# An encoder's first stage: small inputs as rows, a sine in another place, and a loop whose order is written out by hand

## The chip, the cores and the metric

The kernel runs on one core of a Trainium2 chip. The core has five engines with queues of their own, here under the names that the profile gives them: TensorE (PE, matmuls; PEld is its loading of weights), VectorE (DVE), ScalarE (ACT), GpSimd (POOL) and SyncE (SP), whose queue issues the loads and stores. The metric is the device time of one execution in microseconds, the median of several runs. A profiled execution is one more run, whose trace gives each instruction's start and duration from the start of the span.

## The reference

Two layers of an encoder on a sequence of 512 positions with a width of 1024, in f32. Each layer gets six modulation vectors from a conditioning vector `c`: shift, scale and gate for the attention half and for the MLP half. `rope` turns parts of queries and keys by angles that come from the positions.

```
c_act = silu(c)
for l in range(2):
    mod = c_act @ w_mod[l] + b_mod[l]              # 6 x 1024
    sh1, sc1, gt1, sh2, sc2, gt2 = split(mod, 6)
    h = rms_norm(x, g_norm_mix[l]) * (1 + sc1) + sh1
    q_d, k_d, v_d, cq, ckv, k_rope = split(h @ w_in[l])      # 1952 columns
    o_dil = dilated_attention(rms_norm(q_d), rms_norm(k_d), v_d, positions)   # 8 heads, bias by distance
    o_mla = latent_attention(cq, ckv, k_rope, positions, ...)                 # 8 heads, rope on 32 dims
    x = x + gt1 * (concat[o_dil, o_mla] @ w_out[l])
    h = rms_norm(x, g_norm_mlp[l]) * (1 + sc2) + sh2
    x = x + gt2 * (relu(h @ w_mlp_in[l]) ** 2 @ w_mlp_out[l])
```

## The kernel before

x lies transposed: eight tiles `xT[j]` of 128 features by 512 positions. To keep f32's precision, each operand of a large product is split in a rounded high part and a low part that is the rest, and three matmuls add up to one product (`mm3`, L240). `load_split` (L229) does this for weights: a load into a buffer `raw` or `zz`, a copy on ScalarE (`wh`, L233) and a subtraction on GpSimd (`wl`, L234). `raw` has three buffers, `zz` two, `wh` and `wl` four each.

The kernel is written as a program in one order. A planner places each engine's instructions by a model of their times, and may move them past each other where the data allow it; the buffers of a tag are handed on as they come free. Three things limit the planner: `keep_in_program_order` holds one instruction behind what stands before it on its engine, `issue_after` puts all that follows on an engine behind an instruction, and inside a `manual_schedule` block the named engines keep the written order. Before, that block names VectorE alone.

The first stage, which the change touches, goes so:

1. Small loads: `c` as a tile `cs` of 128 x 8, an identity matrix, `cols` (biases and gains), the positions `posc` as 128 x 4, the rotary frequencies `inv`, then the eight tiles of x (L86 to L99).
2. silu of c, with an exponential on ScalarE (L107), spread to all 128 partitions as `cb` by two matmuls and two copies (L111 to L118).
3. The sum of squares of x: ScalarE squares (L124, L127), VectorE adds (L128).
4. Sine and cosine of the rotary angles: thirteen operations on GpSimd reduce the angles (L135 to L145), ScalarE takes an absolute value, GpSimd turns it into the cosine's argument, and ScalarE takes two sines (L150, L151). Then ScalarE's tables for logarithm and exponential are loaded again (L152), and every later instruction of ScalarE stands behind that.
5. The chunk loop (L750 to L780) over the eight chunks k of 128 features. For each chunk two modulation blocks, k (shift) and 8 + k (scale), of 128 x 1024 are multiplied by `cb` and summed on VectorE (`mod_block`, L170), ScalarE adds the biases (`first_norm`, L194 and L195), VectorE multiplies x by the norm's factor `y` (`u_of`, L768 and L759), ScalarE makes the high part of h (L772) and, in a second pass, the unrounded h (L773). The low part of h is a subtraction, for even chunks on VectorE (L763), for odd ones on GpSimd (L775). Every second chunk loads weights of two groups, `win` (768 columns) and `winc` (832 columns). TensorE adds each chunk's 24 matmuls to eight accumulators: 128 x 384 of the first pair of heads, 128 x 416 of the latent projections, for four blocks of positions.
6. The norm's factor (`inv_rms`, L249): TensorE sums over partitions into `p` (L753), VectorE makes a scaled copy `v` (L251), ScalarE takes logarithm (L252) and exponential (L253, over `p`), and three operations of VectorE refine it (L254 to L256).
7. Behind the loop: the norms of q and k (`do_chain`), the turning by TensorE (`tail`), the same for the latent part with the tables of the rotary part (`rope_tables`, L504, and L554 to L562, ten plus four operations on GpSimd and two loads), and the tables of position differences (`distances`, L309). Then eight stages of heads follow (`heads`), where the matmuls of the next stage are woven in by numbers in `TUNE`.

Of the kernel before, what the change touches and what calls it, by code (L numbers as in the profile page):

```python
# [16 lines left out]
L = 2  # L17
D = 1024
# [24 lines left out]
def trunk(ctx: ExitStack, tc: tile.TileContext, a):  # L43
# [42 lines left out]
    cs = col(8, "cs")  # L86
    SY.dma_start(cs, a["c"].rearrange("(k p) -> p k", p=128))
    ident = const.tile([128, 128], F32, name="ident")
    SY.dma_start(ident, a["ident"])
    cols = [col(N_COL, f"cols{l}") for l in range(L)]  # L90
    SY.dma_start(cols[0], a["cols"][0])
    posc = const.tile([128, 4], I32, name="posc")
    SY.dma_start(posc, a["pos"].rearrange("(t p) -> p t", p=128))
    inv = col(16, "inv")
# [9 lines left out]


    e = small(8)
    A.activation(e, cs, AF.Exp, scale=-1.0)  # L107
    V.tensor_scalar(e, e, 1.0, None, op0=OP.add)
    V.reciprocal(e, e)
    V.tensor_tensor(cs, cs, e, op=OP.mult)  # L110
# [20 lines left out]
    pf = col(4, "pf")  # L131
    V.tensor_copy(pf, posc)
    ang, kf, w_ = s2([128, 4, 16]), s2([128, 4, 16]), s2([128, 4, 16], tag="b")
# [12 lines left out]
    A.activation(kf, ang, AF.Abs)  # L146
    G.tensor_scalar(kf, kf, -1.0, math.pi / 2, op0=OP.mult, op1=OP.add)
    sin = const.tile([128, 4, 16], F32, name="sin")
    cos = const.tile([128, 4, 16], F32, name="cos")
    A.activation(sin, ang, AF.Sin)  # L150
    A.activation(cos, kf, AF.Sin)  # L151
    pre = A.preload_act_table_set("natural_log_exp_and_others")  # L152
    tc.keep_in_program_order(pre)
    ctx.enter_context(tc.issue_after(pre.ins))
# [94 lines left out]
    def inv_rms(p, v, y, t):  # L249

        V.tensor_scalar(v, p, 1.0 / D, EPS, op0=OP.mult, op1=OP.add)  # L251
        A.activation(t, v, AF.Ln)  # L252
        A.activation(p, t, AF.Exp, scale=-0.5)  # L253
        V.tensor_tensor(t, v, p, op=OP.mult)  # L254
        V.scalar_tensor_tensor(t, t, -0.5, p, op0=OP.mult, op1=OP.mult)
        V.scalar_tensor_tensor(y, t, 1.5, p, op0=OP.add, op1=OP.mult)  # L256
# [52 lines left out]
    def distances():  # L309
# [3 lines left out]
        part = []  # L313
        for src, n, tile_ in ((posr, S, lambda dt: t4("pt", [128, 2, S], dt)),
                              (posc, 4, lambda dt: const.tile([128, 2, 4], dt, name=nm("pc")))):
            it, ft = tile_(I32), tile_(F32)
            V.tensor_scalar(it[:, 0], src, 16, None, op0=OP.arith_shift_right)
            V.tensor_scalar(it[:, 1], src, 65535, None, op0=OP.bitwise_and)
            V.tensor_copy(ft, it)
            part.append(ft)  # L320
        row, clm = part
# [66 lines left out]
    for l in range(L):  # L388
# [131 lines left out]
        def latent():  # L520
# [20 lines left out]
            def tail():  # L541
                cn = lat["cn"]
                lat["CT"] = []
                for i in range(3):
# [8 lines left out]
                    lat["CT"].append(ct)  # L553
                lat["Cq"], lat["Sq"] = rope_tables(a["gqr"][l], 0)  # L554
# [9 lines left out]
            w["tail"] = tail  # L564
# [169 lines left out]
        if l == 0:  # L734
# [15 lines left out]
            with tc.manual_schedule(engines={mybir.EngineType.DVE}):  # L750
                for k in range(-1, 8):
                    if k < 0:
                        T.matmul(p, ones, sq0, start=True, stop=True)  # L753
                    elif k % 2 == 0:
                        PR[0]["load"][k // 2](raw=("raw", "zz")[k // 2 % 2])
                        W["load"][k // 2](raw=("raw", "zz")[k // 2 % 2])
# [7 lines left out]
                    if k < 7:  # L764
                        mod_block(0, k + 1, "ot", out=mraw[:, k + 1:k + 2])
                        if k < 0:
                            inv_rms(p, v, y, t)
                            V.tensor_tensor(u_of(0), xT[0], y, op=OP.mult)  # L768
# [5 lines left out]
                        if k % 2 == 0:  # L774
                            G.tensor_tensor(lo, u_of(k + 1), f(hi), op=OP.subtract)  # L775
                    if k >= 0:
                        for tb in range(4):
                            PR[0]["step"](banks[tb][:, :384], k, tb)
                        for tb in range(4):
                            W["step"](lbanks[tb][:, :W_C], k, tb)  # L780
            gains()
# [12 lines left out]
        else:  # L794
# [9 lines left out]
            run(ev + [(tn("W0"), PR[0]["tail"][0]), (tn("W1"), PR[0]["tail"][1]), (tn("W2"), W["tail"])])  # L804

        for st in range(8):
# [19 lines left out]
            if st == 7:  # L826
                ev += spread([lambda jj=jj: out_load(1, jj) for jj in range(4)], tn("OL0"), tn("OL1"))
                ev += [(tn("OE") + j, lambda j=j: early(j)) for j in range(3)]
            if l == 0:
# [159 lines left out]
```

## Time and profile before

| | |
|---|---|
| median of 3 runs | 1345.82 us (1344.32 to 1347.77) |
| the profiled execution | 1343.71 us |
| its span | 1341.6 us |
| TensorE busy in the span | 1263.8 us, 94% |
| VectorE, ScalarE, GpSimd busy | 57%, 51%, 49% |
| moved by the DMA queues | 167.62 MB, mean 125 GB/s |
| mean granted clock of TensorE | 0.984 |

A line of a timeline gives start and duration in us, the engine, the line of the kernel, the operation, what is written and read, shapes, the count of merged instructions, and in brackets the idle time before it with what ended it. A line of a group gives busy us and mean ns of one behind the first bar, and idle us with what ended most of it behind the second. A line by stretch gives the stretch, its length, busy us (count) of PE, PEld, DVE, ACT and POOL, then granted clock, DMA share and GB/s.

### The profile page before, as it was taken

How to read it: one execution, taken by the hardware profiler on the slowest of the kernel's cores; microseconds unless marked ns; L12 is line 12 of the kernel's file. 1: busy time of each engine (PE TensorE's matmuls, PEld its weight loads, DVE VectorE, ACT ScalarE, POOL GpSimd, SP SyncE). 2: the span in 40 equal slices, each digit the busy share in tenths (PEclk: the TensorE clock that was granted, in tenths of full speed). 3: DMA queues.
4: the chain of work that ended last, by engine and by line, in shares of the span. 5: the costliest groups of instructions: out<-in, count | busy, mean ns of one | idle time of the engine just before them, and what ended most of it. 6: DMA issues, size and time to landing. Idle time of an engine off the chain costs nothing.

```text
span 1341.6 us, 19641 instructions
## 1 busy us (share of the span) xinstructions
PE 1263.8 (94%) x7114; PEld 1108.2 (83%) x7114; DVE 762.4 (57%) x1644; ACT 679.8 (51%) x1421; POOL 652.0 (49%) x504
## 2 busy tenths in 40 slices
PE   4879988988999999999999999899899999999998
PEld 2878867877998888888899999798799888888888
DVE  6777797886763661834476678987672121121223
ACT  5567898777632322322237677887663232232321
POOL 5646876674534444444438333545452444444441
PEclk7989999999999999999999999999999999999999
DMA  9335543332254572844434244211121222232221
GB/s 340 113 100 174 184 156 110 105 122 69 79 176 166 192 250 95 278 166 161 166 121 131 77 135 123 86 48 63 40 72 64 95 95 96 96 106 96 94 95 64
DMA packets 57248, 167.62 MB, mean 125 GB/s; under 512 B 8640, under 2 KB 10816, under 8 KB 57152
## 3 DMA queue, kind: packets, MB, share of 16 engines
q1 hardware_dynamic: 57152, 166.38, 37.2%
q8 instruction: 56, 0.92, 0.3%
q14 instruction: 40, 0.33, 0.1%
HBM read 155.87 MB, written 10.49 MB: 124 GB/s over the span
## 4 chain that ended last, share of the span: by engine, by line
PE 75%; DVE 6%; ACT 5%; DMA 3%; POOL 3%; issue 2%; DVEq 0%; ACTq 0%; POOLq 0%
PE mm L241 22%; PE mm L244 22%; PE mm L245 22%; PE tr L377 3%; PE tr L365 2%; DMA raw<-in_wout_dram 1%; DVE pt L371 1%; POOL wl L234 1%; DVE P L350 1%; ACT P L354 1%; PE sc L241 1%; ACT wh L233 1%; POOL raw L167 1%; PE sc L244 1%; PE sc L492 1%
## 5 line engine op out<-in xcount | busy, mean ns | idle before, releaser
L234 POOL TENSOR_TENSOR wl<-raw,wh 128x1024 fp32r<-128x1024 f32 (+3 forms) x174 | 395.2, 2273 | 434.4 <-ACT wh L233 431.1
L233 ACT ACTIVATE wh<-raw 128x1024 fp32r<-128x1024 f32 (+3 forms) x174 | 174.7, 1004 | 264.7 <-PE mm L245 212.0
L670 DVE SCALAR_TENSOR_TENSOR x<-mm,mod,x 128x512 f32<-128x512 f32 (+1 forms) x152 | 92.4, 621 | 255.1 <-PE mm L245 254.5
L241 PE MATMUL mm<-h,wh 128*128 128x512 f32 (+1 forms) x544 | 198.3, 364 | 0.0
L244 PE MATMUL mm<-h,wl 128*128 128x512 f32 (+1 forms) x544 | 198.1, 364 | 0.0
L245 PE MATMUL mm<-h,wh 128*128 128x512 f32 (+1 forms) x544 | 197.9, 364 | 0.0
L241 PE MATMUL mm<-ot,wh 128*128 128x512 f32 (+1 forms) x416 | 147.1, 354 | 0.8 <-DVE x L670 0.4
L865 ACT ACTIVATE P<-mm 128x512 f32<-128x512 f32 (+1 forms) x80 | 41.0, 513 | 210.3 <-PE mm L245 206.8
L245 PE MATMUL mm<-ot,wh 128*128 128x512 f32 (+1 forms) x416 | 143.7, 349 | 1.5 <-POOL ot L663 1.5
L244 PE MATMUL mm<-ot,wl 128*128 128x512 f32 (+1 forms) x416 | 144.9, 349 | 0.0
L866 DVE SCALAR_TENSOR_TENSOR mm<-mm,P 128x512 f32<-128x512 f32 (+1 forms) x80 | 46.9, 589 | 135.7 <-ACT P L865 135.7
L241 PEld LDWEIGHTS mm<-h,wh 128*128 128x128 f32 x544 | 102.7, 189 | 16.3
L244 PEld LDWEIGHTS mm<-h,wl 128*128 128x128 f32 x544 | 102.7, 189 | 16.1
L245 PEld LDWEIGHTS mm<-h,wh 128*128 128x128 f32 x544 | 102.6, 189 | 16.2
L241 PE MATMUL mm<-qk,wh 128*128 128x512 f32 (+1 forms) x288 | 105.3, 366 | 1.0 <-DVE x L670 1.0
L244 PE MATMUL mm<-qk,wl 128*128 128x512 f32 (+1 forms) x288 | 105.3, 365 | 0.0
L245 PE MATMUL mm<-qk,wh 128*128 128x512 f32 (+1 forms) x288 | 105.2, 365 | 0.0
L170 DVE SCALAR_TENSOR_TENSOR pt<-pt,cb 128x1024 f32<-128x1024 f32 x56 | 100.7, 1828 | 0.0
L371 DVE TENSOR_TENSOR pt<-tr,pt 128x512 fp32r<-128x512 f32 x128 | 86.6, 684 | 18.1 <-ACT pt L370 17.5
L362 POOL TENSOR_SCALAR P<-P,hs 128x512 f32<-128x512 f32 x64 | 48.1, 751 | 99.9 <-DVE hs L355 81.0
L241 PE MATMUL mm<-wh,h 128*128 128x384 f32 x240 | 81.3, 353 | 11.7 <-ACT h L772 9.8
L365 PE MATMUL tr<-ident,P 128*128 128x128 f32 x512 | 77.5, 275 | 15.7 <-DVE o L381 6.1
(290 smaller groups left out, 2968.9 us busy)
## 6 DMA issues: line engine op xcount, KB each, us to landing
raw<-in_w_dram SPq DMA_DIRECT2D x64, 512.0 KB, 3.4
pt<-in_wmod_dram SPq DMA_DIRECT2D x56, 512.0 KB, 4.8
raw<-in_w2a_dram SPq DMA_DIRECT2D x48, 512.0 KB, 3.5
raw<-in_wmod_dram SPq DMA_DIRECT2D x24, 512.0 KB, 3.6
raw<-in_win_dram SPq DMA_DIRECT2D x30, 384.0 KB, 3.0
bias<-b SPq DMA_DIRECT2D x32, 256.0 KB, 2.1
raw<-in_wout_dram SPq DMA_DIRECT2D x16, 512.0 KB, 3.7
raw<-in_w2b_dram SPq DMA_DIRECT2D x16, 512.0 KB, 3.4
```

Source lines behind the costliest of these rows:

```text
L170: r = V.scalar_tensor_tensor(w, w, 1.0, cb, op0=OP.mult, op1=OP.mult, accum_out=out)
L233: ra = A.activation(hi, raw, AF.Copy)
L234: rg = G.tensor_tensor(lo, raw, f(hi), op=OP.subtract)
L241: r = T.matmul(out, sh, mh, start=first, stop=False)
L244: T.matmul(out, sl, mh, start=False, stop=False)
L245: T.matmul(out, sh, ml, start=False, stop=last)
L362: G.tensor_scalar(P, P, r_, 0.0, op0=OP.mult, op1=OP.add)
L365: T.transpose(tr[:, kc], P[:, kc * 128:(kc + 1) * 128], ident)
L371: V.tensor_tensor(lo, tr, f(hi), op=OP.subtract)
L670: V.scalar_tensor_tensor(xT[j][:, hf], p, gt[:, j:j + 1], xT[j][:, hf], op0=OP.mult, op1=OP.add)
L865: A.activation(r, p, AF.Relu)
L866: V.scalar_tensor_tensor(p, p, 0.0, r, op0=OP.max, op1=OP.mult)
```

## The change

The small inputs `c` and positions are loaded as rows (8 x 128 and 4 x 128, one partition per row) and turned by TensorE, through a PSUM bank; the split of the positions into two halves is done on the rows and turned with them, and `distances` no longer does it. The tables for logarithm and exponential are loaded at the start and a second time behind the chunk loop, by `exp_tables`. The cosine's argument is made by two operations on VectorE, sine and cosine are one operation on ScalarE, and it stands in the chunk loop at k = 0. The logarithm of `inv_rms` reads the sum `p` itself. `manual_schedule` names VectorE, GpSimd, ScalarE and SyncE. The first pair of weight loads moves behind the norm's factor. The rotary part of the latent tail becomes an event of its own, in the first layer at place 2 of the second stage of heads. In `distances` two pairs of buffers become one, with the conversion in place.

```diff
@@ -83,15 +83,15 @@
         return const.tile([128, n], F32, name=nm(name))
-    cs = col(8, "cs")
-    SY.dma_start(cs, a["c"].rearrange("(k p) -> p k", p=128))
-    ident = const.tile([128, 128], F32, name="ident")
+    rows = s2([8, 4, 128], tag="b")
+    crow, prow, pi = rows[:, 0], rows[:4, 1].bitcast(I32), rows[:4, 2:].bitcast(I32)
+    cs, ident, inv = col(8, "cs"), col(128, "ident"), col(16, "inv")
+    cols = [col(N_COL, f"cols{l}") for l in range(L)]
+    SY.dma_start(crow, a["c"].rearrange("(k p) -> k p", k=8))
     SY.dma_start(ident, a["ident"])
-    cols = [col(N_COL, f"cols{l}") for l in range(L)]
+    SY.dma_start(prow, a["pos"].rearrange("(t p) -> t p", t=4))
     SY.dma_start(cols[0], a["cols"][0])
-    posc = const.tile([128, 4], I32, name="posc")
-    SY.dma_start(posc, a["pos"].rearrange("(t p) -> p t", p=128))
-    inv = col(16, "inv")
     SY.dma_start(inv, bass.AP(tensor=a["inv"].tensor, offset=a["inv"].offset, ap=[[0, 128], [1, 16]]))
     xT = [const.tile([128, S], F32, name=f"x{j}") for j in range(8)]
@@ -102,12 +102,20 @@
     epsc = col(1, "eps")
     V.memset(epsc, EPS)
+    def exp_tables():
+        pre = A.preload_act_table_set("natural_log_exp_and_others")
+        tc.keep_in_program_order(pre)
+        ctx.enter_context(tc.issue_after(pre.ins))
+    exp_tables()
     e = small(8)
-    A.activation(e, cs, AF.Exp, scale=-1.0)
+    turn = ps("mm")
+    T.transpose(turn[:, :8], crow, ident[:8, :8])
+    A.activation(e, turn[:, :8], AF.Exp, scale=-1.0)
     V.tensor_scalar(e, e, 1.0, None, op0=OP.add)
     V.reciprocal(e, e)
-    V.tensor_tensor(cs, cs, e, op=OP.mult)
+    V.tensor_tensor(cs, turn[:, :8], e, op=OP.mult)
     cb = const.tile([128, D], F32, name="cb")
     for i in range(2):
         p = ps("sc", (128, 4, 128))
@@ -128,9 +136,22 @@
             V.tensor_tensor(sq0, sq0, sq, op=OP.add)
-    pf = col(4, "pf")
-    V.tensor_copy(pf, posc)
-    ang, kf, w_ = s2([128, 4, 16]), s2([128, 4, 16]), s2([128, 4, 16], tag="b")
+    clm = const.tile([128, 3, 4], F32, name="clm")
+    parts = s2([4, 3, 128], tag="b")
+    V.tensor_copy(parts[:, 2], prow)
+    V.tensor_scalar(pi[:, 0], prow, 16, None, op0=OP.arith_shift_right)
+    V.tensor_scalar(pi[:, 1], prow, 65535, None, op0=OP.bitwise_and)
+    V.tensor_copy(parts[:, :2], pi)
+    turn = ps("mm")
+    for i in range(3):
+        T.transpose(turn[:, 4 * i:4 * i + 4], parts[:, i], ident[:4, :4])
+    V.tensor_copy(clm, turn[:, :12].rearrange("p (i t) -> p i t", i=3))
+    pf = clm[:, 2]
+    sines = const.tile([128, 2, 4, 16], F32, name="sines")
+    sin, cos = sines[:, 0], sines[:, 1]
+    ang, kf, w_ = sin, cos, s2([128, 4, 16])
     for t in range(4):
         G.tensor_scalar(ang[:, t], inv, pf[:, t:t + 1], 0.0, op0=OP.mult, op1=OP.add)
     G.tensor_scalar(kf, ang, 1.0 / (2 * math.pi), 12582912.0, op0=OP.mult, op1=OP.add)
@@ -143,15 +164,8 @@
         G.tensor_tensor(ang, ang, w_, op=OP.add)
     PI_ = 3.1415925
     G.tensor_scalar(ang, ang, PI_, -PI_, op0=OP.min, op1=OP.max)
-    A.activation(kf, ang, AF.Abs)
-    G.tensor_scalar(kf, kf, -1.0, math.pi / 2, op0=OP.mult, op1=OP.add)
-    sin = const.tile([128, 4, 16], F32, name="sin")
-    cos = const.tile([128, 4, 16], F32, name="cos")
-    A.activation(sin, ang, AF.Sin)
-    A.activation(cos, kf, AF.Sin)
-    pre = A.preload_act_table_set("natural_log_exp_and_others")
-    tc.keep_in_program_order(pre)
-    ctx.enter_context(tc.issue_after(pre.ins))
+    V.scalar_tensor_tensor(cos, sin, -1.0, sin, op0=OP.mult, op1=OP.min)
+    V.tensor_scalar(cos, cos, math.pi / 2, None, op0=OP.add)
@@ -248,8 +262,8 @@
     def inv_rms(p, v, y, t):
+        A.activation(t, p, AF.Ln, bias=epsc, scale=1.0 / D)
         V.tensor_scalar(v, p, 1.0 / D, EPS, op0=OP.mult, op1=OP.add)
-        A.activation(t, v, AF.Ln)
         A.activation(p, t, AF.Exp, scale=-0.5)
         V.tensor_tensor(t, v, p, op=OP.mult)
         V.scalar_tensor_tensor(t, t, -0.5, p, op0=OP.mult, op1=OP.mult)
@@ -310,15 +324,11 @@
         posr = s2([128, S], I32)
         SY.dma_start(posr, bass.AP(tensor=a["pos"].tensor, offset=a["pos"].offset, ap=[[0, 128], [1, S]]))
-        part = []
-        for src, n, tile_ in ((posr, S, lambda dt: t4("pt", [128, 2, S], dt)),
-                              (posc, 4, lambda dt: const.tile([128, 2, 4], dt, name=nm("pc")))):
-            it, ft = tile_(I32), tile_(F32)
-            V.tensor_scalar(it[:, 0], src, 16, None, op0=OP.arith_shift_right)
-            V.tensor_scalar(it[:, 1], src, 65535, None, op0=OP.bitwise_and)
-            V.tensor_copy(ft, it)
-            part.append(ft)
-        row, clm = part
+        it = t4("pt", [128, 2, S], I32)
+        V.tensor_scalar(it[:, 0], posr, 16, None, op0=OP.arith_shift_right)
+        V.tensor_scalar(it[:, 1], posr, 65535, None, op0=OP.bitwise_and)
+        row = it.bitcast(F32)
+        V.tensor_copy(row, it)
         V.tensor_scalar(clm[:, 0], clm[:, 0], -65536.0, None, op0=OP.mult)
         dist = [t4("ot", [128, 2, S], F32) for _ in range(2)]
         for qb in range(4):
@@ -551,6 +561,8 @@
                     A.activation(ct[:, 0], src, AF.Copy, scale=g)
                     V.scalar_tensor_tensor(ct[:, 1], src, g, f(ct[:, 0]), op0=OP.mult, op1=OP.subtract)
                     lat["CT"].append(ct)
+            def rope():
                 lat["Cq"], lat["Sq"] = rope_tables(a["gqr"][l], 0)
                 Ck, Sk = rope_tables(a["gkr"][l], 1)
                 krot = lat["krot"] = rot(4)
@@ -561,7 +573,7 @@
                 G.tensor_tensor(t1[:, :, 1], kv_[:, :, 0], Sk[:, :, 1], op=OP.mult)
                 G.tensor_tensor(krot, krot, t1, op=OP.add)
-            w["tail"] = tail
+            w["tail"], w["rope"] = tail, rope
             return w
         def mla_prep(pr):
@@ -747,11 +759,12 @@
             def h_of(k):
                 return hh[k // 2][:, k % 2], hl[k // 2][:, k % 2]
-            with tc.manual_schedule(engines={mybir.EngineType.DVE}):
+            with tc.manual_schedule(engines={mybir.EngineType.DVE, mybir.EngineType.Pool, mybir.EngineType.Activation,
+                                           mybir.EngineType.SP}):
                 for k in range(-1, 8):
                     if k < 0:
                         T.matmul(p, ones, sq0, start=True, stop=True)
-                    elif k % 2 == 0:
+                    elif k % 2 == 0 and k:
                         PR[0]["load"][k // 2](raw=("raw", "zz")[k // 2 % 2])
                         W["load"][k // 2](raw=("raw", "zz")[k // 2 % 2])
                     if k < 7:
@@ -765,6 +778,8 @@
                         mod_block(0, k + 1, "ot", out=mraw[:, k + 1:k + 2])
                         if k < 0:
                             inv_rms(p, v, y, t)
+                            PR[0]["load"][0](raw="raw")
+                            W["load"][0](raw="raw")
                             V.tensor_tensor(u_of(0), xT[0], y, op=OP.mult)
                         first_norm(k + 1)
                         hi, lo = h_of(k + 1)
@@ -773,11 +788,14 @@
                         A.activation(u_of(k + 1), u_of(k + 1), AF.Identity, bias=be, scale=ga)
                         if k % 2 == 0:
                             G.tensor_tensor(lo, u_of(k + 1), f(hi), op=OP.subtract)
+                    if k == 0:
+                        A.activation(sines, sines, AF.Sin)
                     if k >= 0:
                         for tb in range(4):
                             PR[0]["step"](banks[tb][:, :384], k, tb)
                         for tb in range(4):
                             W["step"](lbanks[tb][:, :W_C], k, tb)
+            exp_tables()
             gains()
             for tb in range(4):
                 PR[0]["do_chain"](tb, banks[tb])
@@ -801,7 +819,7 @@
             ev = []
             for n, (w, tb) in enumerate(((PR[0], 0), (PR[0], 1), (W, 0), (W, 1), (PR[0], 2), (PR[0], 3), (W, 2), (W, 3))):
                 ev += spread(w["mm"][tb], 4 * n, 4 * n + 3.6) + [(4 * n + 3.8, w["chain"][tb])]
-            run(ev + [(tn("W0"), PR[0]["tail"][0]), (tn("W1"), PR[0]["tail"][1]), (tn("W2"), W["tail"])])
+            run(ev + [(tn("W0"), PR[0]["tail"][0]), (tn("W1"), PR[0]["tail"][1]), (tn("W2"), W["tail"]), (tn("W2"), W["rope"])])
         for st in range(8):
             ev = []
@@ -826,6 +844,8 @@
             if st == 7:
                 ev += spread([lambda jj=jj: out_load(1, jj) for jj in range(4)], tn("OL0"), tn("OL1"))
                 ev += [(tn("OE") + j, lambda j=j: early(j)) for j in range(3)]
+            if l == 0 and st == 1:
+                ev += [(2, W["rope"])]
             if l == 0:
                 on_dve = ("MV0", "MV1", "MV2", "MV3") if st < 3 else ("MV4", "MV5") if 4 <= st < 7 else ()
                 on_pool = ("MP0", "MP1") if 4 <= st < 7 else ()
```

## The prediction

> **What bounds the kernel now.** I read the page first, then busy time by stretch, then the timelines of single engines, then what waits for whom and the groups of instructions inside the chunk loop.
>
> ```profile
> span 1341.6 us, 19641 instructions
> PE 1263.8 (94%) x7114; PEld 1108.2 (83%) x7114; DVE 762.4 (57%) x1644; ACT 679.8 (51%) x1421; POOL 652.0 (49%) x504
> ```
>
> Over the whole span TensorE is the bound: 94% busy. Little of the work is dated by anything but what precedes it, so what the first stage saves should arrive at the end, unless a later wait takes it. The first stage is another matter. The table by stretch (busy us and count of each engine, then granted clock, DMA share, GB/s) is cut where its limits change: the norm's sum, the first chunk's matmul, the end of the saturated loads, the last product on VectorE, the loop's last matmul, and the next dense run of matmuls.
>
> ```profile
> 14.17:25.73 11.56, 2.07 (x2) 0.50 (x2) 6.64 (x11) 7.15 (x13) 5.73 (x5) 0.50 1.03 410
> 25.73:42.10 16.37, 15.14 (x73) 14.68 (x74) 16.06 (x18) 9.80 (x16) 9.67 (x5) 0.89 0.95 373
> 42.10:59.43 17.33, 14.24 (x66) 12.82 (x65) 16.29 (x25) 9.93 (x17) 9.10 (x9) 0.90 0.12 37
> 59.43:70.49 11.06, 10.62 (x57) 9.89 (x55) 1.36 (x4) 5.21 (x14) 10.10 (x11) 1.00 0.22 62
> 70.49:80.51 10.02, 5.05 (x23) 3.89 (x23) 8.66 (x25) 7.54 (x35) 3.28 (x2) 0.83 0.43 134
> ```
>
> Three things are to be seen. Between 14 and 26 us TensorE does 2 of 11.6 us. From 25.7 to 59.4 VectorE is busy 32.4 of 33.7 us: it paces the loop. Then VectorE stops and GpSimd, busy 10.1 of 11.1 us, holds the end. A matmul of the loop costs 10.62/57 = 0.186 us.
>
> **The head of the loop.** ScalarE, then VectorE and TensorE:
>
> ```profile
> 15.78 1.28 ACT L150 ACT_TABLE_LOAD   x1
> 17.07 0.26 ACT L150 ACTIVATE sin<-s 128x64 f32<-128x64 f32 x1
> 17.49 1.28 ACT L152 ACT_TABLE_LOAD   x1
> 20.00 0.61 ACT L252 ACTIVATE b<-b 128x512 f32<-128x512 f32 x1
> 21.31 0.57 ACT L253 ACTIVATE sc<-b 128x512 f32<-128x512 f32 x1
> 24.86 0.81 ACT L772 ACTIVATE h<-pt,mod,am 128x512 fp32r<-128x512 f32 x1 [2.98 <-DVE pt L768]
> 14.03 1.34 DVE L170 SCALAR_TENSOR_TENSOR qk<-qk,cb 128x1024 f32<-128x1024 f32 x1
> 16.48 0.68 DVE L251 TENSOR_SCALAR b<-sc 128x512 f32<-128x512 f32 x1
> 21.97 0.69 DVE L254 TENSOR_TENSOR b<-b,sc 128x512 f32<-128x512 f32 x1 [4.81 <-ACT sc L253]
> 24.14 0.69 DVE L768 TENSOR_TENSOR pt<-x,P 128x512 f32<-128x512 f32 x1
> 14.17 2.08 PE L753 MATMUL sc<-o,ones 128*128 128x512 f32 x2 [5.35 <-DVE o L128]
> 25.73 1.65 PE L241 MATMUL mm<-wh,h 128*128 128x384 f32 x4 [9.49 <-ACT h L772]
> ```
>
> The norm's sum is there at 14.17 + 2.08 = 16.25, its scaled copy v at 17.16. The logarithm starts only at 20.00, behind the sine, two table loads and a weight copy, and the exponential ends at 21.88; VectorE stands idle for 4.81 us. The change lets the logarithm read the sum itself (16.3 to 16.9). The exponential overwrites that sum, so it waits for v: 17.2 to 17.8. The three operations L254 to L256 took 24.14 - 21.97 = 2.17 us, so the first chunk's product starts at 20.0 instead of 24.14: **-4.1 us**.
>
> Nothing else in the head gets ahead of that, because v stands on VectorE behind the two modulation products that end at 16.48. Even if c and positions as rows let x land earlier, little is won. The nearest rows:
>
> ```profile
> 6.84 0.63 ACT L124 ACTIVATE o<-x 128x512 f32<-128x512 f32 x1 [3.42 <-DMA x<-in_xT_dram]
> 9.58 0.58 ACT L118 ACTIVATE cb<-sc 128x512 f32<-128x512 f32 x1
> 73.42 0.30 PE L479 MATMUL mm<-ident,pt 128*128 128x128 f32 x1 [2.93 <-ACT mm L223]
> ```
>
> The added transposes (0.30 us each as in the last row) stand before the exponential of c and thus before cb, which is ready at 10.16; its first reader starts at 14.03. They and the position split (seven small operations on VectorE instead of five) have 3.9 us of cover; if it were gone they would cost about 1 us. I take 0, ends -0.5 (x earlier) to +1.0.
>
> **The loop.** VectorE's order is the same list as before. Its groups from 24 to 59.5 us (busy, mean ns of one, then idle), two unhindered instructions and one hindered, GpSimd's pair beside it, and GpSimd's groups of the same stretch:
>
> ```profile
> L170 DVE SCALAR_TENSOR_TENSOR qk<-qk,cb 128x1024 f32<-128x1024 f32 x7 | 11.5, 1646 | 0.0
> L170 DVE SCALAR_TENSOR_TENSOR ot<-ot,cb 128x1024 f32<-128x1024 f32 x7 | 9.6, 1372 | 0.0
> L759 DVE TENSOR_TENSOR pt<-x,P 128x512 f32<-128x512 f32 x7 | 9.1, 1303 | 0.0
> L763 DVE TENSOR_TENSOR h<-pt,h 128x512 fp32r<-128x512 f32 x4 | 4.1, 1032 | 1.3 <-ACT pt L773 1.3
> 24.75 0.68 DVE L759 TENSOR_TENSOR pt<-x,P 128x512 f32<-128x512 f32 x1
> 28.31 2.32 DVE L759 TENSOR_TENSOR pt<-x,P 128x512 f32<-128x512 f32 x1
> 58.17 1.25 DVE L170 SCALAR_TENSOR_TENSOR ot<-ot,cb 128x1024 f32<-128x1024 f32 x1
> 27.81 4.68 POOL L234 TENSOR_TENSOR wl<-zz,wh 128x768 fp32r<-128x768 f32 x2 [4.11 <-ACT wh L233]
> L234 POOL TENSOR_TENSOR wl<-zz,wh 128x768 fp32r<-128x768 f32 (+1 forms) x3 | 7.5, 2510 | 4.1 <-ACT wh L233 4.1
> L234 POOL TENSOR_TENSOR wl<-raw,wh 128x768 fp32r<-128x768 f32 (+1 forms) x2 | 4.4, 2222 | 4.2 <-ACT wh L233 4.2
> L775 POOL TENSOR_TENSOR h<-pt,h 128x512 fp32r<-128x512 f32 x3 | 5.4, 1812 | 8.6 <-ACT pt L773 8.6
> ```
>
> The same product takes 0.68 us alone and 2.32 us beside a GpSimd subtraction: the two take turns. At 1.25 and 0.68 us the 25 instructions would need 14 x 1.25 + 11 x 0.68 = 25.0 us; they took 34.3, so GpSimd's work inside the loop costs VectorE 9.3 us. Before, four weight subtractions and the start of a fifth (3 + 2 in the groups), three subtractions of h and five small table products of the rotary part fall into VectorE's stretch. With the hand order these are five weight subtractions (the second of the first pair, and the pairs of chunks 2 and 4), the same three of h, and no table product unless the planner puts it there: about the same. So VectorE's stretch of 59.42 - 24.14 = 35.3 us carries over. New in it is the sine on ScalarE after chunk 1's second pass: a table load of 1.28 plus about 0.3 (0.26 for half as many columns), and behind it the norm of chunk 2 and the weight copies of chunk 2, which GpSimd waits for. VectorE is hit only through its wait for ScalarE's second pass in every other chunk. Ends 0 and +1.6; I take **+0.6**. The last product then ends at 20.0 + 35.3 + 0.6 = 55.9.
>
> [...]
>
> The loads by hand put the last pair's weights before the last two modulation blocks, and those weights wait for GpSimd to free two buffers in the second pair of chunks, by 20.0 + 2 x 10.1 = 40 us (10.1 us a pair, see rival 2). What is queued behind that wait is two weight loads and two modulation blocks, 128 x (768 + 832 + 2 x 1024) x 4 bytes = 1.9 MB. At the 373 GB/s of the table they take 5 us, to 45, and VectorE wants the first of the two blocks at 55.9 - 2 x 1.25 - 0.68 = 52.7: cost 0, and if the buffers came 8 us later, as much as they were late beyond that.
>
> **The end of the loop.** GpSimd and TensorE:
>
> ```profile
> 58.31 4.75 POOL L234 TENSOR_TENSOR wl<-zz,wh 128x768 fp32r<-128x768 f32 x2
> 63.02 0.32 POOL L511 TENSOR_TENSOR rot<-cos,gr 128x64 f32<-128x64 f32 x1
> 64.15 1.84 POOL L234 TENSOR_TENSOR wl<-raw,wh 128x768 fp32r<-128x768 f32 x1
> 65.94 1.28 POOL L775 TENSOR_TENSOR h<-pt,h 128x512 fp32r<-128x512 f32 x1
> 70.14 0.35 PE L245 MATMUL tr<-wl,h 128*128 128x416 f32 x1
> ```
>
> Chunk 7's low part comes at 67.2, behind four table products and the split of the next group's weights (63.02 to 65.94), and the loop ends at 70.49, 11.1 us after VectorE's last product. By hand only the last pair's two subtractions stand before it: free of VectorE at 55.9, the first is done after 1.84, at 57.7, the low part at 55.9 + 1.84 + 1.99 + 1.28 = 61.0 (the second, of 832 columns, is a twelfth longer). TensorE then has 16 matmuls of chunk 6 and 24 of chunk 7 left at 57.7: 40 x 0.186 = 7.4, ending at 65.1. From the low part it would be 61.0 + 16 x 0.186 = 64.0, so the backlog decides. The tail is 9.2 us instead of 11.1: **-1.9**. The loop ends at 65.1 instead of 70.49.
>
> **Behind the loop.** The reload of the exponential's tables (1.28) stands in the tail, where ScalarE was busy 5.21 of 11.06 us and waits for the last matmuls; without that cover, +1.3. The position split needs one big buffer less; 0, ends -1 to 0. The rotary part moves to the second stage of heads: ten table products, four more and two loads of 16 KB on the queue.
>
> ```profile
> 84.41 0.46 POOL L559 TENSOR_TENSOR rot<-kr,rot 128x128 f32<-128x128 f32 x1 [10.64 <-DVE kr L536]
> 130.19 0.70 POOL L362 TENSOR_SCALAR P<-P,hs 128x512 f32<-128x512 f32 x1 [7.96 <-DVE hs L355]
> ```
>
> Fourteen at the 0.32 us of the row at 63.02 are 4.5 us. GpSimd has gaps of 10.6 and 8.0 us there to take them; on the path they delay a bias sum or a normalization of heads. Ends 0 and +4.5; nearest the gaps, I take **+0.4**.
>
> Sum: -4.1 + 0.6 - 1.9 + 0.4 = -5.0. The profiled execution took 1343.71 us (span 1341.6), 2.1 under the median 1345.82; the forecast against the median is **1340.8 us**.
>
> **Rivals.** (1) More than this: the ten microseconds behind the loop shorten too. TensorE is busy 5.05 of 10.02 us there, and 2.93 of that idle stands before the 73.42 row. If the planner orders ScalarE better with the weight copies already out of the way, up to 4 us go: 1337. Against it: the same chain of squares, logarithm and exponential runs there.
> (2) The loop eats the head's gain. From first product to last there are 3.5 pairs of chunks, 35.3/3.5 = 10.1 us each. The hand order makes ScalarE copy the pair's weights only behind the previous chunk's second pass, GpSimd waits for the copies, and VectorE for GpSimd. The loop ends at 20.0 + 3.5 T + 9.2; no gain is left at T = 11.8: 1345.8. For it speaks that five weight subtractions must now come in time; against it that each took its turn before as well.
> (3) The other side: these turns become strictly serial. Per pair, VectorE's 4 x 1.25 + 3 x 0.68 = 7.0, GpSimd's 1.84 + 1.99 + 1.28 = 5.1, and ScalarE's two copies, each at least the 0.81 us of a 512-column pass, 1.6, add to 13.7: the loop ends at 77.2, 6.7 us late, with the rotary part's 0.4 in all 1353. It is slower than before from T = 11.8 on. Against it: the copies of weights need neither VectorE nor GpSimd.
> (4) The change doesn't do what it says: cos now needs two VectorE operations behind GpSimd's reduction of the angles (the sine's tables were loaded at 15.78, right behind it). If they stand before v and GpSimd is late by the 4 us that the logarithm saves, the head's gain is gone: 1345.
>
> **How the numbers follow.** Chances: the forecast 0.52 (its own range 1337 to 1344, from the ends of the sine, the small loads and half of the rotary part), rival 1 0.20, rival 2 0.13, rival 3 0.09, rival 4 0.06. The range reaches from 1333 (rival 1 with no cost for sine and rotary part, and three more from the loop) to 1348 (rival 2 with half of the rotary part on the path); rival 3 and a larger gain are left out. What this measurement can tell from no change is 0.3%, 4 us: faster means under 1341.8. Two thirds of the forecast's cases and rival 1 lie there: 0.34 + 0.20 = 0.54. Rival 3 and the worst of rival 2 are slower: 0.13. The rest, 0.33, is the same.
>
> **What would show it.** Logarithm at about 16.3 and first product at about 20.0; first loop matmul at about 21.6; last modulation product at about 56; last loop matmul at about 65, and the dense run after it at about 75.5. The prediction is wrong if VectorE waits for GpSimd before v, if a pair of chunks takes over 11 us, if the last two modulation blocks land after VectorE asks for them, or if the time from the loop's end to the end of the span changes by more than 2 us.

## The result: 1% slower, and the profile after

The changed kernel takes 1360.09 us (median of 4 runs, 1358.86 to 1361.35) against 1345.07 us for the kernel before on the same chip: a ratio of 1.0104 (95% interval 1.0085 to 1.0124). Ratios below, too, are against the kernel before, timed beside on the same chip. The forecast was 1340.8 us with a range of 1333 to 1348. Its profiled execution took 1358.86 us, with a span of 1357.0 against 1341.6.

The first stage did nearly what was forecast. This is the changed kernel's timeline of the stage, ScalarE first, then VectorE, GpSimd and TensorE (line numbers are those of the changed kernel: logarithm L265, first product L783, sine L792, low part of h L790):

```profile
10.84 0.58 ACT L126 ACTIVATE cb<-sc 128x512 f32<-128x512 f32 x1
15.80 0.69 ACT L265 ACTIVATE b<-sc,eps 128x512 f32<-128x512 f32 x1 [3.35 <-PE sc L766]
28.61 1.28 ACT L792 ACT_TABLE_LOAD   x1
29.91 0.31 ACT L792 ACTIVATE sines<-sines 128x128 f32<-128x128 f32 x1
13.55 0.18 DVE L168 TENSOR_SCALAR sines<-sines 128x64 f32<-128x64 f32 x1
13.65 1.22 DVE L184 SCALAR_TENSOR_TENSOR qk<-qk,cb 128x1024 f32<-128x1024 f32 x1
20.04 1.00 DVE L783 TENSOR_TENSOR pt<-x,P 128x512 f32<-128x512 f32 x1
56.31 1.22 DVE L184 SCALAR_TENSOR_TENSOR ot<-ot,cb 128x1024 f32<-128x1024 f32 x1
41.55 1.44 POOL L525 TENSOR_TENSOR rot<-sines,gr 128x64 f32<-128x64 f32 x1
61.13 0.31 POOL L521 TENSOR_TENSOR rot<-sines,gr 128x64 f32<-128x64 f32 x1
62.46 1.28 POOL L790 TENSOR_TENSOR h<-pt,h 128x512 fp32r<-128x512 f32 x1
66.68 0.35 PE L259 MATMUL tr<-wl,h 128*128 128x416 f32 x1
71.46 0.30 PE L489 MATMUL mm<-ident,pt 128*128 128x128 f32 x1 [4.42 <-DVE pt L479]
```

The first product starts at 20.04 instead of 24.14, and the loop's last matmul ends at 67.03 (66.68 + 0.35) instead of 70.49. The first head of the first layer still ends 2.6 us earlier than before, the fourth 5.0 us.

The time is lost after that, in stages that no line of the diff touches. Here are both kernels by stretch, cut at the same places of the work: end of the chunk loop, end of the first head, of the 5th, 9th, 13th and 16th head, then from the second layer's 15th head to the start of its MLP. The columns are the stretch, its length, busy us (count) of PE, PEld, DVE, ACT and POOL, granted clock, DMA share, GB/s. Before:

```profile
70.50:117.00 46.50, 36.70 (x192) 33.25 (x193) 38.53 (x101) 34.76 (x101) 25.54 (x22) 0.89 0.41 130
117.00:181.20 64.20, 60.85 (x378) 57.28 (x376) 50.88 (x121) 49.53 (x113) 42.64 (x32) 0.97 0.53 169
181.20:245.10 63.90, 53.21 (x343) 44.23 (x343) 51.84 (x139) 54.53 (x135) 44.49 (x51) 0.95 0.38 123
245.10:303.50 58.40, 52.97 (x319) 44.69 (x319) 47.93 (x111) 45.19 (x106) 42.89 (x50) 1.00 0.37 118
303.50:331.20 27.70, 24.12 (x168) 20.99 (x169) 18.35 (x38) 20.70 (x43) 12.54 (x10) 1.00 0.17 58
957.10:1003.30 46.20, 43.99 (x360) 43.48 (x361) 31.72 (x79) 27.76 (x58) 23.13 (x19) 1.00 0.25 80
117.00:331.20 214.20, 191.15 (x1208) 167.18 (x1207) 169.01 (x406) 169.95 (x392) 142.55 (x143) 0.98 0.39 127
```

After:

```profile
67.00:114.30 47.30, 35.38 (x192) 32.23 (x192) 37.10 (x100) 34.45 (x99) 24.70 (x18) 0.91 0.41 131
114.30:179.20 64.90, 60.09 (x372) 55.44 (x371) 48.83 (x116) 49.53 (x111) 43.92 (x37) 0.99 0.50 161
179.20:247.50 68.30, 57.29 (x345) 48.90 (x344) 53.14 (x137) 56.04 (x138) 43.36 (x51) 0.88 0.40 122
247.50:314.50 67.00, 58.71 (x331) 50.76 (x330) 51.34 (x121) 45.89 (x108) 43.02 (x52) 0.90 0.34 111
314.50:343.80 29.30, 25.69 (x166) 21.96 (x166) 17.71 (x36) 19.97 (x41) 11.87 (x9) 0.94 0.18 55
970.70:1018.50 47.80, 45.42 (x357) 44.71 (x358) 30.40 (x75) 26.32 (x56) 21.29 (x16) 0.96 0.23 77
114.30:343.80 229.50, 201.78 (x1209) 177.06 (x1208) 171.02 (x407) 171.42 (x394) 142.17 (x148) 0.92 0.38 122
```

Read the last row of each. From the end of the first head to the end of the 16th it is 229.5 instead of 214.2 us, 15.3 more. The span grew by 15.4: the 2.6 us saved ahead of these heads are lost again behind them, 1.6 of them in the stretch of the second layer (47.8 instead of 46.2). TensorE runs the same matmuls (1,208 and 1,209 records), but is busy 201.8 instead of 191.2 us (+10.6), and idle 27.7 instead of 23.1 (+4.7). Matmuls got slower: the granted clock is 0.92 instead of 0.98. From the 9th to the 13th head it fell from 1.00 to 0.90 and the stretch grew by 8.6 us.

What a stall does there is seen at 250 us of the changed kernel. ScalarE and TensorE, then three stretches around it:

```profile
250.65 1.06 ACT L247 ACTIVATE wh<-raw 128x1024 fp32r<-128x1024 f32 x1 [1.27 <-DMA raw<-in_wout_dram]
248.57 0.40 PE L258 MATMUL sc<-qk,qk 96*128 96x512 f32 x1
248.81 0.39 PE L259 MATMUL sc<-qk,qk 96*128 96x512 f32 x1
252.91 0.79 PE L255 MATMUL sc<-qk,qk 96*128 96x512 f32 x1 [2.84 <-ACT P L364]
253.50 0.63 PE L258 MATMUL sc<-qk,qk 96*128 96x512 f32 x1
253.93 0.63 PE L259 MATMUL sc<-qk,qk 96*128 96x512 f32 x1
250.07:252.91 2.84, 0.00 (x2) 0.00 (x1) 0.69 (x2) 2.27 (x6) 1.13 (x1) 0.94 0.00 1
252.91:259.40 6.49, 6.49 (x22) 5.61 (x23) 5.92 (x20) 5.28 (x17) 4.80 (x8) 0.50 0.28 81
259.40:266.00 6.60, 6.60 (x40) 5.75 (x39) 3.97 (x10) 4.47 (x9) 3.54 (x9) 1.00 0.27 79
```

ScalarE waits 1.27 us for a weight load, which it copies from 250.65 on; the scores' exponential (L364) comes behind that copy, at 252.08, and TensorE waits for the exponential. At 252.57, in the 2.84 us in which TensorE stands still, its granted clock falls to 0.50, for 6.8 us ("half clock" from here on): the same 96x512 matmul takes 0.63 us where it took 0.39, and the next one starts 0.43 us behind it (253.50 to 253.93) instead of 0.24 (248.57 to 248.81). 22 matmuls pass in 6.49 us where 40 passed in the next 6.60, though their shapes are not quite the same. So this stall cost its own 2.8 us and, by an estimate from these starts, some 3 more. In the heads of the changed kernel 32.5 us of TensorE's busy time fall at half clock, before 7.6. If half of the difference is lost, an estimate that is a little high by the same starts, that is 12.4 us; with the 4.7 us of idle time it makes 17.1, where 15.3 were measured.

### The profile page after: what moved, and what is told of

Its sections match the earlier page's. It is cut to its first block, busy times and chain, and to the rows that moved or that the text cites. A ratio compares the mean times of both kernels' runs of the same rounds, so it can differ in the third digit from the quotient of the medians.

```text
span 1357.0 us, 19645 instructions
## 1 busy us (share of the span) xinstructions
PE 1277.1 (94%) x7118; PEld 1121.1 (83%) x7118; DVE 763.9 (56%) x1647; ACT 680.9 (50%) x1419; POOL 651.5 (48%) x503
## 4 chain that ended last, share of the span: by engine, by line
PE 74%; ACT 5%; DVE 5%; DMA 4%; POOL 3%; issue 2%; POOLq 0%; ACTq 0%; DVEq 0%
PE mm L255 21%; PE mm L258 21%; PE mm L259 21%; PE tr L387 3%; PE tr L375 2%; DMA raw<-in_wout_dram 2%; POOL wl L248 1%; DMA bias<-b 1%; PE sc L255 1%; POOL b L356 1%; DMA raw<-in_wup_dram 1%; PE sc L258 1%; PE sc L259 1%; DVE pt L381 1%; ACT pt L380 1%
## 5 line engine op out<-in xcount | busy, mean ns | idle before, releaser
L375 PE MATMUL tr<-ident,P 128*128 128x128 f32 x512 | 81.3, 285 | 14.5 <-DVE pt L381 6.4
L372 POOL TENSOR_SCALAR P<-P,hs 128x512 f32<-128x512 f32 x64 | 45.3, 708 | 91.6 <-DVE hs L365 71.8
L259 PEld LDWEIGHTS mm<-ot,wh 128*128 128x128 f32 x416 | 78.5, 190 | 12.9 <-POOL ot L675 2.7
```

The source lines that it names most:

```text
L259: T.matmul(out, sh, ml, start=False, stop=last)
L372: G.tensor_scalar(P, P, r_, 0.0, op0=OP.mult, op1=OP.add)
L375: T.transpose(tr[:, kc], P[:, kc * 128:(kc + 1) * 128], ident)
```

## The experiments

Theory A: the rotary part's move is what costs, by what it does to the heads. Rival B: the new first stage shifts or overloads what follows. Under A there are two mechanisms. C: the planner orders the heads in another way once the position differences are written ahead of the rotary part, and that order stalls more. D: the moved operations themselves get in the way there.

**1. The rotary part back in the latent tail**, all else as changed.

```diff
-            def rope():
...
-            if l == 0 and st == 1:
-                ev += [(2, W["rope"])]
```

> The changed kernel with the rotary part back in the latent tail, ahead of the position differences; everything else of the change stays. Theory A (the loss comes from writing the rotary part behind the position differences, which makes the planner lay out the first layer's heads anew): the first stage's gain of 3 to 5 us is left, 1339 to 1343 us, TensorE at half clock for about 10 us between 95 and 350 us as before (37.5 us in the changed kernel). Theory B (the hand order of the loop shifts the plan, and the heads lose whatever the rotary part does): 1352 to 1360 us, 30 us or more at half clock.

The heads of this kernel by stretch:

```profile
113.90:332.50 218.60, 196.07 (x1209) 172.31 (x1208) 171.10 (x407) 170.24 (x392) 144.42 (x143) 0.95 0.39 127
```

Measured: 1344.56 us (1342.44 to 1347.53), ratio 0.9991 (0.9977 to 1.0005). The loss is gone, so A, just above its range. The heads took 218.6 us, still 4.4 more than before, with 23.9 us of half clock between 95 and 350 us instead of the expected 10 or so.

**2. The kernel before with the rotary part's move alone.**

```diff
+            def rope():
...
+            if l == 0 and st == 1:
+                ev += [(2, W["rope"])]
```

> The kernel before with the rotary part alone moved to the second stage of heads. Theory A: about 1358 to 1362 us, the heads of the first layer 13 to 16 us later at their end, 30 us or more at half clock between 95 and 350 us. Theory B: 1344 to 1348 us, about 10 us at half clock.

Measured: 1355.06 us (1352.09 to 1359.48), ratio 1.0073 (1.0047 to 1.0100); the heads took 224.8 us at a clock of 0.94. The move is enough for two thirds of the loss; the expected 1358 was too high.

**3. The kernel before with the hand order on four queues, the first weight loads moved, and the logarithm from the sum**; the sine stays ahead of the loop.

```diff
+            with tc.manual_schedule(engines={mybir.EngineType.DVE, mybir.EngineType.Pool, mybir.EngineType.Activation,
+                                           mybir.EngineType.SP}):
...
+        A.activation(t, p, AF.Ln, bias=epsc, scale=1.0 / D)
```

> The kernel before with the hand order on four engines (with the first weight loads behind the norm's factor) and the logarithm reading the sum itself; sine, small loads, position split and rotary part as before. Theory A: the heads keep their order, so only the head of the loop changes. The sine still stands on ScalarE ahead of the logarithm, which starts at about 19 us, so 1 to 3 us of gain: 1342 to 1345 us. Theory B: 1350 us or more.

Measured: 1348.12 us, ratio 1.0019 (1.0004 to 1.0034). Missed by both theories. The head of the loop did gain: the logarithm started at 17.32 and the first product at 21.63, 2.5 us earlier than before.

```profile
21.63 1.00 DVE L771 TENSOR_TENSOR pt<-x,P 128x512 f32<-128x512 f32 x1
66.94 1.29 POOL L778 TENSOR_TENSOR h<-pt,h 128x512 fp32r<-128x512 f32 x1
```

The end of the loop lost it. Chunk 7's low part started only at 66.94, behind five table products and four weight subtractions, two of them for the group after the loop; the loop ended at 73.01 instead of 70.49, and the first head 2.1 us later than before.

**4. The changed kernel with the hand order on VectorE alone.**

```diff
+            with tc.manual_schedule(engines={mybir.EngineType.DVE}):
```

> The changed kernel with the hand order on VectorE alone. Both theories: the heads stay as in the changed kernel, so still 1352 us or more. If the hand order is worth what the prediction gave it (the 1.9 us at the loop's end, less what the planner does better), the loop's last matmul comes 0 to 4 us later than in the changed kernel, 1360 to 1364 us; if the planner orders these engines better than the hand, 1355 to 1359 us.

Measured: 1359.26 us, ratio 1.0104 (1.0072 to 1.0135), between the two ranges. The first head ended 2.2 us earlier than before, against 2.6 with all four queues: the hand order on ScalarE, GpSimd and for the loads buys 0.4 us there and does not make the loss. The head of the loop looks quite different, though:

```profile
15.20 0.31 ACT L791 ACTIVATE sines<-sines 128x128 f32<-128x128 f32 x1
17.10 0.69 ACT L265 ACTIVATE b<-sc,eps 128x512 f32<-128x512 f32 x1
23.60 0.69 DVE L782 TENSOR_TENSOR pt<-x,P 128x512 f32<-128x512 f32 x1
```

Left free, the planner put the sine ahead of the logarithm again and loaded tables three times (at 13.91, 15.81 and 19.50); the first product came at 23.60 instead of 20.04. By the end of the loop (68.45) only 1.4 us of that were left.

**5, 6 and 7. The order of the heads held.** For these three, the first layer's heads get edges that hold each queue's instructions in the order that the planner had chosen for another kernel; what each instruction does is unchanged, and no semaphore is added. Shortened:

```diff
+        for e in queues:
+            for r in order_of_the_other_kernel[e]:      # place of an instruction of the heads on this queue
+                tc.add_manual_dep(mine[r], prev.name, NoSync)
```

5 is kernel 2 (rotary part moved alone) with the heads in before's order; the moved operations are left free, as they are in 6, the changed kernel with the heads in before's order. 7 is the kernel before with its heads in the changed kernel's order.

> The kernel before with the rotary part moved, as in the run of that alone, but with the first layer's heads held, on each of the five queues, to the order that the planner gave them in the kernel before. Theory C (the loss is the order alone): 1343 to 1347 us, no loss left, about 10 us at half clock between 95 and 350 us. Rival D (the rotary part's own work, its place among the heads and the buffers it now takes later cost the time): 1352 to 1357 us as without holding.

> The changed kernel with the first layer's heads held to the order of the kernel before. Theory C: the first stage's gain comes through, 1339 to 1343 us. Rival D: 1355 us or more. A third outcome, 1344 to 1348 us: the order is the loss, and the first stage's gain is eaten by waits where the held order no longer fits the earlier start.

> The kernel before, with the first layer's heads held to the order that the planner gave them in the changed kernel; the rotary part and the first stage are as before. Theory C: the loss without the change, 1356 to 1364 us, 25 us or more at half clock between 95 and 350 us. Rival D: 1344 to 1349 us.

The heads of kernels 2, 5, 6 and 7 by stretch, from the end of the first to the end of the 16th:

```profile
116.30:341.10 224.80, 198.37 (x1209) 174.86 (x1208) 169.00 (x406) 170.96 (x394) 141.31 (x148) 0.94 0.39 124
116.30:331.50 215.20, 193.21 (x1209) 169.87 (x1208) 169.50 (x407) 170.18 (x391) 143.77 (x146) 0.96 0.39 127
114.90:329.30 214.40, 194.01 (x1209) 170.53 (x1208) 168.82 (x407) 170.18 (x391) 143.76 (x146) 0.95 0.39 127
116.20:339.00 222.80, 197.06 (x1205) 172.98 (x1204) 169.88 (x406) 171.13 (x394) 139.60 (x144) 0.94 0.38 124
```

Measured: 5 took 1347.44 us, ratio 1.0008 (0.9997 to 1.0018): C, though 0.4 us above its range; once the order is held, the moved operations cost nothing that this measurement can tell from zero. 6 took 1345.90, ratio 1.0007 (0.9995 to 1.0019): the third outcome, the changed kernel without its loss and without its gain. Its heads took 214.4 us, as before, and every head from the first to the 16th ended 1.7 to 2.1 us early; behind the heads that was given back. 7 took 1354.34, ratio 1.0066 (1.0049 to 1.0083): the order alone, put on the kernel before, lengthened the heads by 8.6 of the 15.3 us, less than C expected. So without the new order there is no loss, and the order by itself brings somewhat more than half of it; what brings the rest together with the order was not tested. The new order is another one indeed: of the 2,379 places of these heads on the five queues, 1,867 differ between the list that 6 holds and the list that 7 holds.

**8 and 9. Another order for another reason.** One number of the weaving, the place of the first modulation block in the first three stages of heads, goes from 1.5 to 1.6, in the kernel before (8) and in the changed one (9).

```diff
-    ... MV0=(1.5,) ...
+    ... MV0=(1.6,) ...
```

> The kernel before with one number of the weaving changed: MV0, the place of the first modulation block in each of the first three stages of heads, 1.6 instead of 1.5. Nothing is computed otherwise, but the planner puts some 1,900 places of the five queues in another order. Theory P (the order of before's heads is a chosen one, and other orders of the same work cost several us, whatever brings them about): 1350 to 1360 us, with 25 us or more of half clock between 95 and 350 us. Rival Q (only the order that the position differences bring about is a bad one): 1343 to 1348, half clock 10 to 17 us.

> The changed kernel with the same number, MV0 1.6 instead of 1.5, which reorders some 1,250 places against the changed kernel. Theory P: somewhere else than 1360, between 1343 and 1362, by what stalls this order happens to have; the time goes with the half clock between 95 and 350 us (37 us there in the changed kernel), about 0.5 us of time for each us of it, beside the idle time of TensorE. Rival Q: within 3 us of the changed kernel's 1360, since the position differences still stand ahead of the rotary part.

```profile
118.70:348.70 230.00, 200.91 (x1214) 178.56 (x1215) 169.38 (x410) 169.45 (x392) 143.88 (x144) 0.93 0.37 121
113.80:346.00 232.20, 200.27 (x1214) 177.33 (x1215) 173.39 (x410) 170.69 (x393) 141.82 (x147) 0.92 0.37 120
```

Measured: 8 took 1362.18 us (1361.15 to 1363.49), ratio 1.0117 (1.0102 to 1.0133), slower than the changed kernel; its heads, above, look like those after, with 37.5 us of half clock between 95 and 350 us. So the rotary part is only one way to lose the order of before, and P holds against Q; it lay above P's own range. 9 took 1358.10, ratio 1.0095 (1.0069 to 1.0122), which both allowed.

**10. The changed kernel with the output weights' loads earlier.**

```diff
-    ... LO=(7.2, 7.2) ...
+    ... LO=(6.2, 7.2) ...
```

> The changed kernel with the loads of the output weights written earlier in the stages of heads: LO 6.2 instead of 7.2 in the first layer, some 690 places away from the changed kernel's order. Two of its half-clock stretches (252.6 and 307.2) follow stalls of 2.84 and 2.66 us in which ScalarE waits for these loads. If the stalls make the half clock, the stalls at 250 and 305 and the half clock behind them go, and 6 to 9 us come back: 1350 to 1354. If the loads are limited by their buffers and not by their place, the stalls stay and the time is 1357 to 1362.

Its heads, and TensorE at the two places:

```profile
113.60:336.60 223.00, 197.50 (x1205) 173.84 (x1204) 172.20 (x407) 170.34 (x394) 142.19 (x148) 0.93 0.38 125
250.18 0.51 PE L255 MATMUL sc<-qk,qk 96*128 96x512 f32 x1 [1.44 <-ACT P L364]
302.90 2.05 PE L387 MATMUL tr<-pt,qk 128*128 128x256 f32 x8 [2.39 <-DVE pt L381]
```

Measured: 1348.68 us, ratio 1.0018 (1.0002 to 1.0034), 11.4 us back, more than expected. The stall of 2.84 us became 1.44 and that of 2.66 became 2.39; the half clock behind the first went from 6.8 to 3.4 us, a stretch of 3.4 us at 328 went away, one at 145 came, and the one behind the second stayed. The heads took 6.5 us less; of the rest, 0.7 us came ahead of them, 1.2 behind them, and 2.9 are the distance of the two profiled runs from their medians. It is again another order (some 690 places), and one of the two stalls hardly changed, so the expected cause is good for a part of this at most, and that more came back than expected is luck.

**11 and 12. Rotary part back, with one thing more**: the hand order on VectorE alone (11), or the earlier loads of 10 (12).

> The changed kernel with the rotary part back in the latent tail and the hand order on VectorE alone, some 2,000 places away from the order of before. The kernel with the rotary part back and four queues by hand took 1344.56. Theory P: the order is one more draw, 1342 to 1356, and the first stage's 2 us at the end of head 0 say nothing of the end. Rival Q: 1341 to 1346, since the position differences stand behind the rotary part again.

> The changed kernel with the rotary part back in the latent tail and the output weights' loads written earlier (LO 6.2), both edits that brought time back; some 800 places away from before's order. With the rotary part back alone: 1344.56, with 23.9 us of half clock between 95 and 350 us, 6.8 of them at 298 behind stalls of 1.4 to 1.9 us at 292 to 299. If that half clock goes with the earlier loads, 3 to 4 us come off: 1340 to 1342. If the order is one more draw without a stall removed: 1343 to 1350.

Measured: 11 took 1349.25, ratio 1.0023 (1.0009 to 1.0038): its first head ended 1.0 us late, and the end is 3 to 4 us above before, as P has it and Q does not. 12 took 1344.44, ratio 0.9992 (0.9979 to 1.0004), the same as with the rotary part back alone; the earlier loads gave nothing there, and the half clock at 297 that they were to remove stayed. No kernel tried was faster than before by more than the measurement can tell.

**What stays open.** Held to the order of before, the changed kernel's 2 us at the end of the heads were no longer there at the end of the span; which of its later stalls took them was not tested, and over the 14 traces the stretch behind the heads takes 1010.4 to 1014.6 us, so that a single trace cannot tell. Nor was the half clock switched off by itself; what it costs is read from the matmuls' durations and starts. Why the order of the changed kernel costs 15.3 us there and 8.6 us in the kernel before is open, and so is which of the instructions that the planner saw first tipped the order.

## Why the prediction was wrong

**Head of the loop, -4.1: right.** The product was forecast at 20.0 and started at 20.04. The cosine's two operations on VectorE, which rival 4 feared, were done at 13.73, as the first modulation product began. But most of the gain rests on the sine's place, not on the logarithm's reading the sum: with the sum read and the sine ahead of the logarithm the first product came at 23.60 in experiment 4 and at 21.63 in experiment 3. With the hand order on all four queues the sine stays behind.

**Small loads and transposes, 0: right.** `cb` was ready at 11.42 instead of 10.16, and its first reader started at 13.65.

**The loop, +0.6: too small by 1.6 us.** The last product ended at 57.53, not 55.9. The sine cost what was taken: 1.28 of table load and 0.31, and it starts right behind the load (29.91). The five table products of the rotary part that were to leave VectorE's stretch are still in it (the row at 41.55, 1.44 us beside VectorE instead of 0.31 alone): the planner took them into the loop although they are written in the second stage of heads. VectorE waited no longer than before (1.1 us instead of 1.3), but its seven products with `y` took 11.0 us instead of 9.1. That GpSimd's five products make the 1.6 us is read from these rows, not tested.

**The end of the loop, -1.9: nearly right.** From the last product to the last matmul it took 9.5 us instead of 11.1, -1.6. The reason given was off: GpSimd's table products stood before chunk 7's low part again (61.13), so that part came at 63.74 and not at 61.0, and it set the end instead of TensorE's backlog. With both, the loop ended at 67.03, 1.9 us later than forecast.

**Behind the loop, 0 and +0.4: the step that failed.** The rotary part was priced at its own 4.5 us of GpSimd and the gaps of GpSimd that would take them. By experiment 5 that price was right, near nothing. It was cheaper than thought: of the fourteen operations that are written in the heads now, the planner ran ten in the loop (38.29 to 62.49) and one at 83.22, as before, so that only three moved.

```profile
83.22 0.84 POOL L571 TENSOR_TENSOR rot<-kr,rot 128x128 f32<-128x128 f32 x1 [11.88 <-DVE kr L546]
127.08 1.31 POOL L572 TENSOR_TENSOR s<-kr,rot 128x64 f32<-128x64 f32 x1
128.36 0.32 POOL L573 TENSOR_TENSOR s<-kr,rot 128x64 f32<-128x64 f32 x1
129.91 0.45 POOL L574 TENSOR_TENSOR rot<-rot,s 128x128 f32<-128x128 f32 x1
```

What the step left out is that the text in front of the planner changes, and with it the planner's order of the heads: 1,867 of 2,379 places. With that the heads took 15.3 us longer, where the step has +0.4. The text moves fourteen operations, the queues move three, and the bill comes with the order of all others.

Ahead of the heads the step was off by little: the table load (59.85) was covered, as taken, but the dense run of matmuls came at 78.48, 11.45 us behind the loop's end instead of 10.02. The row that fits is a weight copy of ScalarE at 68.61, which waited 1.31 us for its load with the norm's exponential behind it; that was not tested.

**The assumption above it**, that what the first stage saves arrives at the end unless a later wait takes it, took the heads as a fixed block that only shifts. The prediction's last part named the sign of its failing: the time from the loop's end to the end of the span was not to change by more than 2 us. It went from 1271.1 to 1290.0.

None of the four rivals was this one. Rival 3, the slow one, looked for the loss inside the chunk loop, where the rows were; of the planner's order of untouched stages the profile of before shows nothing but a clock of 0.98 in the heads and 23 us of idle time, and the question that was not asked is whether that is a property of the work or of one order. Experiments 2, 7, 8 and 9 say of the order: over the kernels tried here the same matmuls take 191 to 202 us of TensorE, with 20 to 32 us of idle time beside.

## What to carry to other kernels

Where a planner sets the order, an edit has two prices: that of its own work, and that of the order it brings about in stages that it does not touch. Compare the planned orders of both kernels before costing anything; where most places differ, the profile of before says little of those stages, and none of the other orders tried here was faster than that of before. To measure the edit itself, hold the untouched stages to the old order: here that turned a ratio of 1.0104 into 1.0007.

## What was not expected of the hardware

The half clock came in steps of 3.413 us. In the clock records of the profiled executions before and after, all stretches at half clock start at whole multiples of 3.413 us from each other, and those that end within the span last one, two, three or five times 3.413 us. The grid of these starts lies 1.2 us further on, counted from the start of the span, in the trace of after than in that of before. The idle time of TensorE was added up in each step of that grid from 95 to 1320 us. Of the two traces' 700 steps at full clock, 10 were followed by half clock: all 7 with over 1.85 us of idle time, 3 of the 12 from 1.25 to 1.85, and none of the 681 with less. The longest gap does not tell the two kinds apart. In the kernel before, a gap of 2.12 us across a border between two steps (113.70 to 115.82) was followed by full clock (1.00 from 111.39 to 118.21), and one of 1.83 us inside a step (142.83 to 144.66) by 3.4 us at 0.50.

```profile
115.82 0.44 PE L479 MATMUL mm<-ident,zz 128*128 128x128 f32 x2 [2.12 <-DVE zz L469]
144.66 0.50 PE L492 MATMUL sc<-qk,qk 128*128 128x512 f32 x1 [1.83 <-DVE hs L350]
142.10:145.52 3.42, 1.59 (x9) 0.89 (x8) 3.42 (x7) 2.21 (x7) 3.42 (x3) 1.00 0.84 222
145.52:148.93 3.41, 3.41 (x17) 3.41 (x17) 2.86 (x11) 2.81 (x7) 2.74 (x3) 0.50 0.84 315
```

Several shorter gaps were followed by half clock too: 0.69 us before 326.42 and 0.85 us before 327.65 in the changed kernel, with 1.53 us of idle time in their step as a whole, by 3.4 us of it from 327.66 on. Such a step at half clock cost some 1.5 us, by an estimate for matmuls as close as those at 250 us: of its 3.4 us, 0.44 is lost by the starts read there (0.43 us apart instead of 0.24). That where a stall falls in the grid is part of why orders that look alike differ was not tested.
